# The second layer's modulation made in the first layer's MLP but for twelve columns, on one Trainium2 core

## The chip, the cores and the metric

One Trainium2 chip, one of its cores. The metric is the time of one execution of the kernel on the device, in microseconds (us), lower is better. Shown are the median of three runs and one further execution taken by the hardware profiler.

## The reference, cut to what matters

Two layers over a sequence of 512 frames of 1024 channels, all in float32. Each layer first makes six vectors of 1024 values from a conditioning vector c, the same for all frames; this is the modulation:

```python
c_act = silu(c)
for l in range(2):
    mod = c_act @ ada_w[l] + ada_b[l]                 # 1024 -> 6 * 1024
    sh1, sc1, gt1, sh2, sc2, gt2 = split(mod, 6)
    h = rms_norm(x, norm1_g[l]) * (1 + sc1) + sh1
    ...                                                # projections of h, RWKV-7 scan, pooling, gates
    x = x + gt1 * (mixed @ w_out[l])
    h2 = rms_norm(x, norm2_g[l]) * (1 + sc2) + sh2
    gate, up = split(h2 @ w_gu[l], 2)
    x = x + gt2 * ((silu(gate) * up) @ w_down[l])
return rms_norm(x, final_g)
```

Of these vectors sh1 and sc1 are needed when a layer begins, gt1 at the end of its mixer (everything up to w_out), sh2 and sc2 at the start of its MLP, gt2 at the MLP's end.

## The kernel before, in words

Channels lie on the 128 partitions, frames along the free dimension: eight tiles of 128 x 512 hold x. Every float32 product runs as three TensorE passes with operands split into a high part rounded to fp32r and a low remainder (`block`, L217): weights come as 128 x 1024 tiles of 512 KB (`weights`, L174), loaded by SyncE's queue into `raw` (three buffers), cast on ScalarE to `whi` (L185), and the remainder `wlo` is made either on VectorE (L191) or, with `by_dma`, by ScalarE writing minus raw (L188) and an accumulating transfer from GpSimd's queue (L189).

**The modulation** of one layer is 48 columns of 128 outputs, numbered 0 to 47 (sh1 0 to 7, sc1 8 to 15, gt1 16 to 23, sh2 24 to 31, sc2 32 to 39, gt2 40 to 47). One column is one row load of 512 KB by SyncE's queue (`rows`, L239) and one VectorE multiply-and-sum over 1024 elements with `cact` (`modulation`, L248, L254), which leaves the sum in `mods`. The profile names such an instruction by where its row landed: `row`, `hf`, `ar` or `raw`.

Columns still to be made stand in the list `self.todo`. `some(n)` (L259) is called at chosen places of the program; each call makes the column that has been on its way longest, if as many rows are on their way as there are landing places (`self.land`), and sends for new rows until all places are filled. `flush` makes what is left on the way. The landing places are borrowed from tiles that stand empty at the time: two `ar` tiles in the mixer until head pair 3 begins to fill them, after that `raw` buffers of the weights themselves, two halves of `hf0` in w_out, two tiles `row0` and `row1` in the MLP and the down products.

**Layer 0** begins with its 16 columns of sh1 and sc1. Its mixer makes the next 24, its w_out 6, and its last two are made in its MLP. The MLP (`mlp`, L1234) has two parts. First 19 steps of about 10 us (`seven`, L1178), in which gate and up projections are made as seven half-size products; `some(1)` stands in every third step (L1346). Then the down products, eight products m of 22 blocks (`product`, L1380), whose results go to x at once (`residual`, L367). For m = 1 to 6 `some(1)` stands after every second group of three blocks, three in a product (L1399 to L1406), behind the residual of product m - 1: `tc.issue_after` puts the block's instructions on that instruction's engine, VectorE, behind it in the engine's order. These places take 25 columns, 2 of layer 0 and 23 of layer 1. The constant LATE = 26 allows 26 to be left, and 25 are. The seventh of the eight products is followed by `onward` (L458): the last product in two halves, and between its blocks the norm of the next stage and that stage's first projections, in a TensorE order that is fixed by the program (`pinned`).

**Layer 1's mixer** (`mixer`, L925) puts the left columns back into `todo` (L932). It projects the pool inputs and, for each head pair j = 0 to 3, k, r and v, then the 16 gates. While head pair j is prepared on VectorE, ScalarE and GpSimd (`front`, L621: decay, normalised keys; `back`, L677: value residual, chunk matrices `ar`), TensorE is given the blocks of the projections in between; the table SLOT (L79) says how many blocks follow which part, and its third number where `some(1)` stands: four times in each of the rounds j = 1 to 4. So 17 columns are made here, the last four of them through `raw` buffers. Then `solve` (L737) inverts 64 x 64 triangles on VectorE under 51 blocks of gates, `chain` (L812) runs the scan. Before w_out what exceeds eight columns is made (L1024), and `gains` (L1026) makes 1 + sc2 times the norm's weight. w_out takes 6 columns, the MLP the last 2.

Engines work off their instructions in the order in which the scheduler put them; a DMA queue does the same, so a load that waits for its buffer holds up the loads behind it.

Of the kernel before, what the change touches and what calls it, by code (L numbers as in the profile page):

```python
# [19 lines left out]
P = 128  # L20
# [46 lines left out]


SOME = 1
LATE = 26  # L70

NORM = ((12, 4), (14, 10))

# [44 lines left out]
class Trunk:  # L118
    def __init__(self, ctx, tc, a, out):
        self.ctx, self.tc, self.nc, self.a, self.out = ctx, tc, tc.nc, a, out  # L120
        self.pinned, self.last, self.by_dma = False, None, False
        self.third, self.turn, self.ahead, self.on_way, self.land = None, 0, 1, [], []
        self.count, self.fetched = 0, []
        self.hf, self.exact, self.later = None, False, []
        nc = self.nc
        pool = lambda **k: ctx.enter_context(self.pool(**k))
        self.const = pool(name="const", bufs=1)
        self.wraw = pool(name="wraw", bufs=3)
        self.whl = pool(name="whl", bufs=2)
        self.hp = pool(name="hp", bufs=1)  # L130
        self.psum = pool(name="psum", bufs=4, space=PSUM)
        self.dram = pool(name="dram", bufs=1, space=DRAM)
        self.cst = self.const.tile([P, N_CST], F32, name="cst")
        self.cols = self.const.tile([P, N_COLS], F32, name="cols")
        self.ones = self.const.tile([P, P], F32, name="ones")
        self.mean = self.const.tile([P, 1], F32, name="mean")
        self.eps = self.const.tile([P, 2], F32, name="eps")
        self.mods = [self.const.tile([P, 48], F32, name=f"mods{l}") for l in range(L)]
        self.gsc = [self.const.tile([P, 16], F32, name=f"gsc{l}") for l in range(L)]
        self.omm = [self.const.tile([P, 15], F32, name=f"omm{l}") for l in range(L)]  # L140
        self.omka = [self.const.tile([P, 4], F32, name=f"omka{l}") for l in range(L)]
        self.xs = [self.dram.tile([P, S], F32, name=f"xs{k}") for k in range(KC)]
        self.yb = {
            (n, g): self.dram.tile([P, S], F32, name=f"{n}{g}") for n in ("yh", "yl") for g in range(4)
        }
        self.vf = [self.dram.tile([P, S], F32, name=f"vf{j}") for j in range(NJ)]
        self.hd = {k: self.dram.tile([P, S], F32, name=f"hd{k}") for k in AWAY}
# [26 lines left out]
    def weights(self, src, engine=None, pool=None, pair=None):  # L174

        nc = self.nc
        raw = self.fetched.pop(0) if self.fetched else self.fetch(src)
        if pool is None:
            pool = self.whl
            if self.third is not None:  # L180
                self.turn = (self.turn + 1) % 3
                pool = self.whl if self.turn else self.third
        new = lambda n: pool.tile([P, 1024], F32R, tag=n, name=n)
        hi, lo = pair() if pair else (new("whi"), new("wlo"))
        self.on(nc.scalar, "copy")(hi, raw)  # L185
        self.count += 1
        if self.by_dma and (self.by_dma is True or self.count % self.by_dma):
            nc.scalar.activation(lo, raw, AF.Copy, scale=-1.0)  # L188
            nc.gpsimd.dma_start(lo, src, accum_op=ALU.add)  # L189
        else:  # L190
            self.on(nc.vector, "tensor_tensor")(lo, raw, hi.bitcast(F32), ALU.subtract)  # L191
        return hi, lo
# [66 lines left out]
    def some(self, n):  # L259

        for _ in range(n):
            ahead = max(1, len(self.land))
            self.flush(ahead - 1)
            while self.todo and len(self.on_way) < ahead:
                l, i = self.todo.pop(0)
                self.on_way.append((l, i, self.rows(l, i)))

# [190 lines left out]
    def onward(self, l, which, xs, soon, late, last, head=NORM[0]):  # L458

        self.new_h()
        a, b = HALVES
        self.go(last(a))
        ws, banks = soon(), None
        self.pinned = True
        under = last(b)
        for hs, n in zip(HALVES, (head, NORM[1])):
            self.go(under, n[0])
            rb = self.rstd(hs, lambda: self.go(under, n[1]))  # L470
            self.go(under)
            for k in range(KC):
                self.modulated(l, which, xs[k], rb, k, hs)
                if banks is None:
                    ws += late()
                    banks = self.banked(ws)
            under = self.outer(banks, ws, hs)
        self.soon(AF.Silu if which else AF.Sigmoid)
        self.go(under)
        self.pinned = False  # L480
        return banks


# [85 lines left out]
    def pooled(self, l, zs, st, fill):  # L569

        nc, tc = self.nc, self.tc
        with self.pool(name="pl", bufs=1, side="right") as pl:
            pw = pl.tile([P, 512], F32, name="pw")
            nc.sync.dma_start(pw, self.a["pool_w"][l])
            for g in range(4):
                ps = zs[g]
                if l == 0:
                    self.some(SOME)
                z = pl.tile([P, PAD + S], F32, tag="z", name="z", bufs=2)
                nc.gpsimd.memset(z[:, 0:PAD], 0.0)  # L580
                nc.scalar.copy(z[:, PAD:], ps)
# [343 lines left out]
    def mixer(self, l):  # L925
# [3 lines left out]
        deep = ExitStack()  # L929
        self.third = deep.enter_context(self.pool(name="third", bufs=1, side="right"))  # L930
        self.turn = 2 * l
        self.todo, self.later = self.todo + self.later, []  # L932
        self.pre = right.enter_context(self.pool(name="pre", bufs=13, side="right"))
        sl = right.enter_context(self.pool(name="sl", bufs=1, side="right"))
        sm = low.enter_context(self.pool(name="sm", bufs=1, side="right"))
# [1 line left out]
        rest = range(POOL0 + len(zs), KRV0)  # L937
        st = self.stream([((self.a["w_in"][l, g],), zs.append) for g in rest], [self.m] * 4)
        self.go(st, KC)
        self.g = self.dram.tile([P, NJ, S], F32, tag="g", name="gd")  # L940
        self.krv = {}

# [18 lines left out]
        with ExitStack() as ctx:  # L961
# [26 lines left out]
            for j in range(NJ + 1):  # L988
                self.by_dma = 2 if j in (2, 3) else True
                if l and j == 2:  # L990
                    self.turn, self.count = self.turn + 1, 1
                if j == NJ:
                    self.flush()
                    self.land = []
                steps = [(self.front(l, j) if j < NJ else iter(()), True), (self.back(l, j - 1) if j else iter(()), False)]
                steps = {ahead: g for g, ahead in steps}
                fill = st if j < NJ - 1 else gates
                for n, ahead, some in SLOT[min(j, 1)]:
                    next(steps[ahead], None)
                    self.go(fill, n)  # L1000
                    if some and (l == 0 or j):
                        self.some(1)
            right.close()
            gp = ctx.enter_context(self.pool(name="gp", bufs=1))
# [18 lines left out]
        self.tmp = self.left.enter_context(self.pool(name="t2", bufs=1))  # L1023
        self.some(len(self.todo) - 8)  # L1024
        self.flush()
        self.gains(l, 1)  # L1026
        with ExitStack() as ctx:
            mx = ctx.enter_context(self.pool(name="mx", bufs=1))
            mixed, outs = [], []
# [24 lines left out]
            self.by_dma, self.ahead = False, 1  # L1054
            self.wide = ExitStack()
            hb = self.wide.enter_context(self.pool(name="hb", bufs=1, side="right"))
            self.hb = self.wide.enter_context(self.pool(name="hc", bufs=1, side="right"))
            self.hf = [p.tile([P, KC // 2, S], F32, name=n) for p, n in ((self.hb, "hf0"), (hb, "hf1"))]
            wo = ctx.enter_context(self.pool(name="wo", bufs=3))
            wk = ctx.enter_context(self.pool(name="wk", bufs=4))  # L1060

# [9 lines left out]
            for m in range(KC):  # L1071
                x = self.xp.tile([P, S], F32, tag=f"x{m}", name="x")
                nc.sync.dma_start(x, self.a["x"][m] if l == 0 else self.xs[m])
                self.x.append(x)
            self.land = [self.hf[0][:, 2 * i : 2 * i + 2, :].rearrange("p k n -> p (k n)") for i in range(2)]
            for m in range(5):
                if m == len(outs):
# [1 line left out]
                self.some(1)  # L1079
                self.go(product(m, outs[m], ALL))  # L1080
            self.flush()
            self.land = []
            w = [wout(m, wo) for m in range(5, KC)]

# [149 lines left out]
    def mlp(self, l):  # L1234
# [7 lines left out]
        fp = right.enter_context(self.pool(name="fp", bufs=2, side="right"))  # L1242
        rows = [fp.tile([P, D], F32, name=f"row{i}", bufs=1) for i in range(2)]
        pairs, ws = [], {}
        x = lambda tag: fp.tile(
            [P, S if tag == "x22" else D], F32, tag=tag, name=tag, bufs=1 if tag == "x13" else 2
        )
# [36 lines left out]
        with ExitStack() as ctx:  # L1284
# [40 lines left out]
            for i, m in [*enumerate(HIDDEN)][PLAIN:]:  # L1325
                s, out = begin(m)

                def at(place):
# [14 lines left out]
                        if made:  # L1343
                            nc.gpsimd.dma_start(*made)
                    elif place == 2:
                        if i % 3 == 0 and i < FC - 3:  # L1346
                            self.some(1)
                        step(i + 1)
                    elif place == 3:
# [24 lines left out]
        for k in AWAY:  # L1374
            nc.sync.dma_start(kept[k], self.hd[k])
        t3 = right.enter_context(self.pool(name="t3", bufs=1, side="right"))
        if self.todo:
            self.land = rows

        def product(m, hs):  # L1380
            ps = self.acc() if hs.start == 0 else self.m()
# [15 lines left out]
                yield  # L1397

        for m in range(KC - 1):  # L1399
            stream = product(m, ALL)  # L1400
            for n in range(6):
                self.go(stream, 3)
                if m and n % 2:
                    with tc.issue_after(self.behind.ins):
                        self.some(1)
            self.go(stream)  # L1406
# [1 line left out]
        if l < L - 1:  # L1408
            self.some(len(self.todo) - LATE)
        self.flush()  # L1410
        self.land = []
        self.later, self.todo = self.todo, []
        if l < L - 1:
            self.gains(l + 1, 0)

            pair = self.hb.tile([P, 2, D], F32R, tag="hf0", name="wn", bufs=1)
            both = mr.tile([P, few * S], F32R, tag="hd", name="wn", bufs=1)
            ahead = [
                self.weights_in(l + 1, 2, both=both[:, 0:D]),
# [9 lines left out]
            self.early = dict(enumerate(banks))  # L1429
            right.close()  # L1430
            left.close()
        else:
            self.go(product(KC - 1, HALVES[0]))
            under = product(KC - 1, HALVES[1])
# [141 lines left out]
```

## Time and profile before

| what | before |
|---|---|
| median of 3 runs | 1508.88 us (1507.56 to 1510.38) |
| the profiled execution | 1512.63 us |
| its span, first to last instruction | 1510.8 us |
| around the span | 1.83 us |
| TensorE matmul busy | 1437.5 us, 95% |
| VectorE busy | 1097.3 us, 73% |
| ScalarE busy | 742.9 us, 49% |
| GpSimd busy | 254.5 us, 17% |
| mean granted TensorE clock | 0.988 |
| moved by DMA | 299.28 MB, mean 198 GB/s |

Layer 0's MLP steps lie at about 450 to 640 us of the span, its down products at 640 to 760, layer 1's mixer at 785 to 1100, its w_out to 1125 and its MLP behind that. PE is TensorE, PEld its weight loads, DVE VectorE, ACT ScalarE, POOL GpSimd, SPq SyncE's queue. A row of a timeline gives the start, the duration, and in brackets how long the engine had been idle just before and what ended that. A matmul of 128 x 512 is listed with some 0.39 us but the next starts 0.23 us later: they overlap.

### The profile page before, as it was taken

What the parts mean: (1) busy time and instruction counts of PE and PEld (TensorE: products, weight loads), DVE (VectorE), ACT (ScalarE), POOL (GpSimd) and SP (SyncE); (2) the same over time, 40 slices, a digit from 0 to 9 for tenths busy, and PEclk for the clock granted to TensorE, in tenths of its full rate; (3) what the DMA queues carried; (4) which work ended last, traced back from release to release, by engine and by line L of the source; (5) the groups of instructions that cost most, each with busy time, mean ns of one, the idle gap of its engine ahead of it and who ended that gap; (6) DMA issues with size and microseconds to landing.
All of it is one profiled execution on the core that took longest, in us unless ns stands there. A gap on an engine that the chain in (4) does not pass through costs nothing. (4 is left out here: it accounts for less than half of the span.)

```text
span 1510.8 us, 25366 instructions
## 1 busy us (share of the span) xinstructions
PE 1437.5 (95%) x9986; PEld 1226.7 (81%) x9986; DVE 1097.3 (73%) x1857; ACT 742.9 (49%) x1014; POOL 254.5 (17%) x296
## 2 busy tenths in 40 slices
PE   4999899999999999999999989899999999999997
PEld 2776677777899999988897757677779999998886
DVE  7789869676788888865675796677577888787333
ACT  4376554343446656632346656353434666656221
POOL 1124321110022211100022333111102122110000
PEclk9999999999999999999999999999999999999998
DMA  9478689698739988766726966876975699885332
GB/s 360 152 243 244 194 216 275 156 267 245 227 103 240 233 204 194 190 210 200 241 67 204 237 180 164 242 188 175 298 244 156 179 218 206 182 168 165 92 97 70
DMA packets 112487, 299.28 MB, mean 198 GB/s; under 512 B 12080, under 2 KB 22704, under 8 KB 112368
## 3 DMA queue, kind: packets, MB, share of 16 engines
q1 hardware_dynamic: 89440, 227.93, 46.1%
q0 software_dynamic: 21776, 68.69, 25.2%
q8 instruction: 78, 1.28, 0.3%
q10 hardware_dynamic: 1152, 1.05, 0.2%
q14 instruction: 41, 0.34, 0.1%
HBM read 269.84 MB, written 27.79 MB: 197 GB/s over the span
## 5 line engine op out<-in xcount | busy, mean ns | idle before, releaser
L211 PE MATMUL acc<-hh,whi 128*128 128x512 f32 (+1 forms) x1128 | 398.4, 359 | 5.3 <-ACT hh L364 4.9
L211 PE MATMUL acc<-hh,wlo 128*128 128x512 f32 (+1 forms) x1120 | 385.4, 349 | 13.0 <-DMA wlo<-in_w_in 10.8
L211 PE MATMUL acc<-hl,whi 128*128 128x512 f32 (+2 forms) x1128 | 375.9, 350 | 2.1 <-POOL hl L365 1.4
L185 ACT CAST whi<-raw 128x1024 fp32r<-128x1024 f32 x151 | 157.8, 1048 | 286.2 <-PE acc L211 186.9
L211 PEld LDWEIGHTS acc<-hh,wlo 128*128 128x128 f32 x1120 | 213.8, 191 | 42.7 <-DMA wlo<-in_w_in 12.9
L211 PEld LDWEIGHTS acc<-hh,whi 128*128 128x128 f32 x1128 | 214.9, 191 | 40.8 <-ACT hh L364 7.8
L211 PEld LDWEIGHTS acc<-hl,whi 128*128 128x128 f32 (+1 forms) x1128 | 207.1, 191 | 30.3 <-POOL hl L365 2.5
L191 DVE TENSOR_TENSOR wlo<-raw,whi 128x1024 fp32r<-128x1024 f32 x86 | 104.9, 1227 | 94.1 <-ACT whi L185 93.7
L211 PE MATMUL acc<-f,whi 128*128 128x512 f32 (+1 forms) x304 | 92.2, 386 | 0.0
L211 PE MATMUL m<-tl,f13h 128*128 128x256 f32 x304 | 86.0, 283 | 0.0
L211 PE MATMUL m<-th,f13l 128*128 128x256 f32 x304 | 86.0, 283 | 0.0
L211 PE MATMUL m<-th,f13h 128*128 128x256 f32 x304 | 85.9, 283 | 0.0
L231 ACT CAST f24h<-x 128x1024 fp32r<-128x1024 f32 x38 | 39.9, 1051 | 61.8 <-DVE x L231 61.8
L188 ACT ACTIVATE wlo<-raw 128x1024 fp32r<-128x1024 f32 x65 | 68.4, 1053 | 0.1
L211 PEld LDWEIGHTS acc<-f,whi 128*128 128x128 f32 x304 | 56.2, 188 | 12.3
L254 DVE CUSTOM_DVE_ANT_0 raw<-raw,cact,cols 128x1024 f32<-128x1024 f32 x29 | 39.8, 1384 | 32.4 <-DMA raw<-in_ada 32.3
L1175 POOL DMA_DIRECT2D f22l<-in_w_gu x38 | 32.7, 861 | 168.4 <-ACT f22l L231 160.0
L189 POOL DMA_DIRECT2D wlo<-in_w_in x41 | 35.8, 873 | 149.9 <-ACT wlo L188 149.9
L231 DVE TENSOR_TENSOR f24l<-x,f24h 128x1024 fp32r<-128x1024 f32 x38 | 46.5, 1224 | 18.9 <-ACT f24h L231 18.9
L211 PE MATMUL acc<-f,wlo 128*128 128x512 f32 (+1 forms) x152 | 58.7, 386 | 0.0
L211 PEld LDWEIGHTS m<-th,f13h 128*128 128x128 f32 x304 | 58.4, 192 | 0.0
L211 PEld LDWEIGHTS m<-th,f13l 128*128 128x128 f32 x304 | 58.4, 192 | 0.0
(319 smaller groups left out, 3437.9 us busy)
## 6 DMA issues: line engine op xcount, KB each, us to landing
raw<-in_w_in SPq DMA_DIRECT2D x70, 512.0 KB, 5.3
raw<-in_w_gu SPq DMA_DIRECT2D x50, 512.0 KB, 4.4
raw<-in_w_down SPq DMA_DIRECT2D x44, 512.0 KB, 3.6
wlo<-in_w_in POOLq DMA_DIRECT2D x41, 512.0 KB, 7.7
wlo<-in_w_gu POOLq DMA_DIRECT2D x40, 512.0 KB, 6.4
x<-in_w_gu SPq DMA_DIRECT2D x76, 256.0 KB, 4.2
raw<-in_ada SPq DMA_DIRECT2D x29, 512.0 KB, 5.4
ar<-in_ada SPq DMA_DIRECT2D x28, 512.0 KB, 5.2
```

The costliest lines, as they stand in the source:

```text
L185: self.on(nc.scalar, "copy")(hi, raw)
L188: nc.scalar.activation(lo, raw, AF.Copy, scale=-1.0)
L189: nc.gpsimd.dma_start(lo, src, accum_op=ALU.add)
L191: self.on(nc.vector, "tensor_tensor")(lo, raw, hi.bitcast(F32), ALU.subtract)
L211: i = (tensor.transpose if transpose else tensor.matmul)(*args, **k).ins
L231: return (lambda *a, **k: self.tc.keep_in_program_order(op(*a, **k))) if self.exact else op
L254: self.on(nc.vector, "tensor_tensor_reduce")(out=raw, in0=raw, in1=self.cact, scale=1.0, scalar=self.cols[:, b + i : b + i + 1], op0=ALU.m ...
L1175: nc.gpsimd.dma_start(lo, two[:, b], accum_op=ALU.add)
```

## The change

- LATE becomes 12, and the list of columns is held at 12 throughout layer 0's MLP by a new number `keep`: `some` sends for no row while 12 or fewer are left.
- In the MLP's steps of layer 0 `some(1)` stands in every second step instead of every third (in layer 1 still every third, from step 5 on).
- In the down products it stands after every group of three blocks but the first, five in a product, for m = 1 to 6, and once in m = 0. From m = 1 there are four landing places: the tile `hf1`, whose contents are used up by then, gives two more. So four rows are on their way.
- In `some` the test is rewritten: a call makes one column if all landing places are filled or nothing more may be sent for, then fills the places.
- The twelve left columns go back into `todo` only at w_out of layer 1 (before: at the start of its mixer). The mixer's `some(1)` of layer 1 thus find nothing. `gains(l, 1)` moves behind the columns of w_out.
- Two weight tiles that layer 1's mixer begins with (`rest`) get their `wlo` behind a marked VectorE instruction of `onward`: the modulation of tile 4 of the norm's second half. Their ScalarE cast is free as before, since the order is set on the marked instruction's engine alone.

```diff
-LATE = 26
+LATE = 12
...
         hi, lo = pair() if pair else (new("whi"), new("wlo"))
+        if self.after:
+            with self.tc.issue_after(self.after.ins):
+                nc.scalar.copy(hi, raw)
+                nc.vector.tensor_tensor(lo, raw, hi.bitcast(F32), ALU.subtract)
+            return hi, lo
...
             ahead = max(1, len(self.land))
-            self.flush(ahead - 1)
-            while self.todo and len(self.on_way) < ahead:
+            if len(self.on_way) >= ahead or len(self.todo) <= self.keep:
+                self.flush(max(0, len(self.on_way) - 1))
+            while len(self.todo) > self.keep and len(self.on_way) < ahead:
...
                 self.modulated(l, which, xs[k], rb, k, hs)
+                if k == 4:
+                    middle = self.behind
...
-        self.todo, self.later = self.todo + self.later, []
...
         self.go(st, KC)
+        self.after = None
...
-                    if some and (l == 0 or j):
+                    if some:
                         self.some(1)
...
         self.some(len(self.todo) - 8)
         self.flush()
-        self.gains(l, 1)
...
+            self.todo += self.later
             self.land = [self.hf[0][:, 2 * i : 2 * i + 2, :].rearrange("p k n -> p (k n)") for i in range(2)]
...
             self.flush()
+            self.gains(l, 1)
...
+        self.keep = LATE if l < L - 1 else 0
...
-                        if i % 3 == 0 and i < FC - 3:
+                        if (i + l) % (2 + l) == 0 and i < FC - 3:
                             self.some(1)
...
         for m in range(KC - 1):
+            if m == 1:
+                more = self.hb[1].tile([P, 2, D], F32, tag="hf1", name="rows", bufs=1)
+                self.land = [more[:, 0, :], more[:, 1, :], *self.land]
             stream = product(m, ALL)
             for n in range(6):
                 self.go(stream, 3)
-                if m and n % 2:
+                if n and (m or n > 4):
                     with tc.issue_after(self.behind.ins):
                         self.some(1)
...
+            self.after = self.middle
```

## Rows read from the trace of the kernel before

**Rows 1.** The profile's page, part 1: busy us, share, instructions, of each engine
```profile
PE 1437.5 (95%) x9986; PEld 1226.7 (81%) x9986; DVE 1097.3 (73%) x1857; ACT 742.9 (49%) x1014; POOL 254.5 (17%) x296
```

**Rows 2.** Busy time by stretch, layer 1's mixer: PE, PEld, DVE, ACT, POOL, clock, DMA
```profile
860.00:880.00 20.00, 14.63 (x92) 10.22 (x92) 19.94 (x25) 7.58 (x11) 9.57 (x9) 0.92 0.83 228
...
960.00:980.00 20.00, 13.93 (x54) 10.97 (x53) 18.84 (x36) 7.78 (x9) 3.70 (x5) 0.83 0.95 250
```

**Rows 3.** Timeline of PE, 850 to 975 us: the rows behind its idle times
```profile
861.40 1.16 PE L211 MATMUL m<-kr,bk 64*128 64x128 f32 x16 [3.06 <-DVE sig L691]
...
877.08 2.05 PE L211 MATMUL m<-sig,cst 128*128 128x512 f32 x2 [3.97 <-DVE sig L666]
...
904.55 1.10 PE L211 MATMUL m<-sig,cst 128*128 128x512 f32 x2 [1.26 <-DVE sig L666]
...
942.24 1.16 PE L211 MATMUL m<-kr,bk 64*128 64x128 f32 x14 [1.13 <-DVE ar L707]
...
955.05 0.50 PE L211 MATMUL acc<-hh,wlo 128*128 128x512 f32 x1 [0.50 <-DMA wlo<-in_w_in]
972.32 0.80 PE L211 MATMUL acc<-hh,wlo 128*128 128x512 f32 x1 [6.07 <-DMA wlo<-in_w_in]
```

**Rows 4.** Instructions of L254, 830 to 965 us: duration ns min/median/max, first and last start
```profile
L254 DVE CUSTOM_DVE_ANT_0 ar<-ar,cact,cols x13: 1268/1280/2284, 839.2 to 907.5; 128x1024 f32<-128x1024 f32 x13
...
L254 DVE CUSTOM_DVE_ANT_0 raw<-raw,cact,cols x4: 1283/1284/1286, 931.9 to 959.7; 128x1024 f32<-128x1024 f32 x4
```

**Rows 5.** Timeline of DVE, 851 to 877 us
```profile
851.42 0.69 DVE L688 TENSOR_TENSOR d<-d,sv 128x512 f32<-128x512 f32 x1 [0.52 <-POOL d L687]
857.64 1.29 DVE L254 CUSTOM_DVE_ANT_0 ar<-ar,cact,cols 128x1024 f32<-128x1024 f32 x1 [5.52 <-DMA ar<-in_ada]
...
876.20 0.73 DVE L666 SCALAR_TENSOR_TENSOR sig<-r,cols,k 128x512 f32<-128x512 f32 x1
```

**Rows 6.** Timelines of SyncE's queue, DVE and ACT, 940 to 964 us
```profile
950.40 10.90 SPq L171 DMA_DIRECT2D raw<-in_w_in  x2
...
959.65 1.28 DVE L254 CUSTOM_DVE_ANT_0 raw<-raw,cact,cols 128x1024 f32<-128x1024 f32 x1 [10.53 <-DMA raw<-in_ada]
...
960.72 1.05 ACT L185 CAST whi<-raw 128x1024 fp32r<-128x1024 f32 x1 [5.98 <-DMA raw<-in_w_in]
```

**Rows 7.** Busy time by stretches of 2 us: the seventh number is the granted clock
```profile
878.00:880.00 2.00, 2.00 (x6) 0.77 (x4) 1.97 (x3) 0.00 (x0) 1.17 (x1) 0.50 1.03 200
...
974.00:976.00 2.00, 2.00 (x6) 1.52 (x6) 1.84 (x5) 0.00 (x0) 0.00 (x0) 0.51 1.09 269
```

**Rows 8.** Layer 0's down products: busy time by stretch; L254 there; loads of weights
```profile
655.00:745.00 90.00, 90.00 (x392) 73.09 (x391) 53.01 (x70) 23.00 (x25) 0.00 (x0) 1.00 0.68 226
...
L254 DVE CUSTOM_DVE_ANT_0 row<-row,cact,cols x20: 1275/1280/1287, 655.5 to 744.7; 128x1024 f32<-128x1024 f32 x20
...
raw<-in_w_down SPq DMA_DIRECT2D x18, 512.0 KB, 4.2
```

**Rows 9.** The closest call of those products: timelines of DVE and ACT, 700 to 707 us
```profile
701.23 1.28 DVE L254 CUSTOM_DVE_ANT_0 row<-row,cact,cols 128x1024 f32<-128x1024 f32 x1
...
703.04 1.22 DVE L191 TENSOR_TENSOR wlo<-raw,whi 128x1024 fp32r<-128x1024 f32 x1
...
700.33 1.05 ACT L185 CAST whi<-raw 128x1024 fp32r<-128x1024 f32 x1 [4.37 <-PE acc L211]
...
705.97 1.05 ACT L185 CAST whi<-raw 128x1024 fp32r<-128x1024 f32 x1 [3.98 <-PE acc L211]
```

**Rows 10.** Busy time by stretch: sixteen steps of the MLP in layer 0 (PE, PEld, DVE, ACT, POOL)
```profile
460.00:620.00 160.00, 160.00 (x1342) 160.00 (x1341) 132.72 (x202) 97.56 (x128) 32.10 (x40) 1.00 0.91 212
```

**Rows 11.** Timelines of DVE and ACT around the norm of layer 1's first stage
```profile
761.12 1.23 DVE L191 TENSOR_TENSOR wlo<-raw,whi 128x1024 fp32r<-128x1024 f32 x1
...
784.50 2.00 ACT L185 CAST whi<-raw 128x1024 fp32r<-128x1024 f32 x2 [4.58 <-PE acc L211]
```

More of the change, by code (lines that the diff above doesn't have):

```diff
@@ L123, in __init__ @@
         self.count, self.fetched = 0, []
-        self.hf, self.exact, self.later = None, False, []
+        self.hf, self.exact, self.later, self.keep = None, False, [], 0
+        self.after = None
         nc = self.nc
@@ L480, in onward @@
         self.pinned = False
+        self.middle = middle
         return banks
@@ L576, in pooled @@
                 ps = zs[g]
-                if l == 0:
-                    self.some(SOME)
+                self.some(SOME)
                 z = pl.tile([P, PAD + S], F32, tag="z", name="z", bufs=2)
@@ L939, in mixer @@
         self.go(st, KC)
+        self.after = None
         self.g = self.dram.tile([P, NJ, S], F32, tag="g", name="gd")
@@ L1056, in mixer @@
             hb = self.wide.enter_context(self.pool(name="hb", bufs=1, side="right"))
-            self.hb = self.wide.enter_context(self.pool(name="hc", bufs=1, side="right"))
-            self.hf = [p.tile([P, KC // 2, S], F32, name=n) for p, n in ((self.hb, "hf0"), (hb, "hf1"))]
+            hc = self.wide.enter_context(self.pool(name="hc", bufs=1, side="right"))
+            self.hb = hc, hb
+            self.hf = [p.tile([P, KC // 2, S], F32, name=f"hf{i}") for i, p in enumerate(self.hb)]
             wo = ctx.enter_context(self.pool(name="wo", bufs=3))
@@ L1376, in mlp @@
         t3 = right.enter_context(self.pool(name="t3", bufs=1, side="right"))
-        if self.todo:
-            self.land = rows
+        self.land = rows
         def product(m, hs):
@@ L1410, in mlp @@
         self.flush()
-        self.land = []
+        self.land, self.keep = [], 0
         self.later, self.todo = self.todo, []
@@ L1414, in mlp @@
             self.gains(l + 1, 0)
-            pair = self.hb.tile([P, 2, D], F32R, tag="hf0", name="wn", bufs=1)
+            pair = self.hb[0].tile([P, 2, D], F32R, tag="hf0", name="wn", bufs=1)
             both = mr.tile([P, few * S], F32R, tag="hd", name="wn", bufs=1)
```

## The prediction

> **What bounds the kernel now.** I began with the page's busy times. TensorE's matmuls are busy 95% of the span, VectorE 73% [rows 1]: seen over the whole span TensorE is the limit, and there are only 1510.8 - 1437.5 = 73 us in which it stands still. So the next view was the busy time by 20 us, to see where those lie. Apart from both ends of the span the MLPs and the down products have none, and layer 1's mixer has the largest: 5.4 us of 860 to 880, where VectorE works 19.94 of 20, and 6.1 us of 960 to 980, where the granted clock is 0.83 as well [rows 2]. In these stretches it isn't TensorE that limits.
>
> The timeline of TensorE names each wait [rows 3]. Four end with a VectorE result: 3.06, 3.97, 1.26 and 1.13, together 9.42 us. Two end when an accumulating weight transfer lands: 0.50 and 6.07. All six have the modulation behind them, in two ways. In the first, VectorE itself: 17 columns are made between 839 and 961 us, 13 through `ar` and 4 through `raw` [rows 4], at 1.28 us each when undisturbed, so 17 x 1.28 = 21.8 us of an engine that works in order; besides, it stood 5.52 us before one of them waiting for its row, with the value residual's L688, begun at 851.42, already behind it [rows 5]. The second is SyncE's queue and the weights' buffers: the last four rows occupy `raw`, of which there are three. A weight load spent until 961.3 in the queue (950.40 + 10.90), the column at 959.65 had kept VectorE idle for 10.53, and the cast at 960.72 waited 5.98 for its load [rows 6]. Cast, remainder and accumulation of that weight are what TensorE then waited for until 972.32.
>
> Idle time has a second price here. Behind the 3.97 us gap the granted clock is 0.50, and behind the 6.07 us one 0.51 [rows 7], the lower of two levels, 1.2 GHz of 2.4; behind the 3.06 us gap I saw no fall. At 0.5 from 877.1 to about 880.3 and from 972.3 to 976.0 TensorE does half the work, so it loses about 1.6 and 1.85 us.
>
> **The change, part by part.**
>
> *Out of the mixer.* All 17 columns leave it: VectorE loses 21.8 us, SyncE's queue 17 issues, the DMA engines 17 x 0.524 = 8.9 MB, and the `raw` ring four tenants. Counting calls: before, MLP and down products of layer 0 made 25 columns and left 25; after, eight calls in the steps take 9, one in m = 0 takes 1, the first of m = 1 takes 2, and 26 more reach 38, with 12 left and three calls over. W_out still takes 6, and layer 1's MLP sends for 6 instead of 2. So of the 17, 13 move to layer 0's MLP and 4 to layer 1's.
>
> The first four waits: at 877.08 the producer is L666 at 876.20, and VectorE's run up to it began 5.52 us late at 857.64 [rows 5], with columns ahead of it and inside it. That wait and any two columns gone make 5.52 + 2.56 = 8.1 us, and TensorE asks for 3.06 + 3.97 = 7.0 up to there. Each further wait has more columns removed ahead of it. I count all 9.42 and the 1.6 of clock: 11.0. Next late, should one remain, would be ScalarE's and GpSimd's links of the same head pair.
>
> The last two waits and their clock are 0.50 + 6.07 + 1.85 = 8.4 us. With `raw` for weights alone the load of 950.40 can go when its buffer's weight is done, and the cast would follow TensorE's release of `whi`. But the chain behind the cast stays (ScalarE twice, GpSimd's issue, an accumulation), and the DMA share is 0.95 [rows 2] and 1.03 to 1.09 in parts [rows 7]. Bounds: 0 to 8.4; I take 5.0, nearer the top since the row load is what came last. Solve's VectorE part starts behind the last column and should gain as much as TensorE.
>
> *Into layer 0's down products.* Eleven more columns: 14.1 us of VectorE in 90, where it is busy 53 [rows 8], so some 67; 5.8 MB on top of 226 GB/s, or 64 GB/s, which at the present ratio of share to rate makes 0.68 x 290 / 226 = 0.87. TensorE there is busy all 90 of 90 [rows 8], and GpSimd's queue is empty. What could suffer is a weight's remainder, which VectorE must finish before the next change of weights. In the closest case the casts start at 700.33 and 705.97, the remainder ended at 704.26, 1.7 us ahead, with one column in front of it [rows 9]. A column more in front costs 1.28, still hidden; two more would show 0.9 us. SyncE's queue carries eleven more loads, each possibly waiting for a column, with weight loads behind it; but a weight lands in 4.2 us [rows 8] and has three buffers of 5.6 us each. Bounds 0 to 20 us (all four landed rows in front of one remainder in each of six products, below); I take 0.5, since the columns stand three blocks apart in the program and a remainder comes every eight.
>
> *Into the MLP steps.* Layer 0 makes two more, layer 1 four more, at 1.28. A step has 84 matmuls, so 1342 of them in 160 us make a step of 10.0 us [rows 10]; VectorE's 132.72 less five columns over 16 steps is 7.9 us. With a column it is 9.2, as in every third step already, with TensorE at 160 of 160. Two fall into layer 1's down products, where nothing else was made. Cost 0; the cover is 0.8 us a step, and past it each costs its overhang.
>
> *The two remainders behind the marked instruction.* One, at 761.12, stood among the norm's steps [rows 11] and goes behind the marked one, some 15 us later by the norm's length. TensorE didn't wait there, so nothing is gained; at most its 1.2 us. Behind it only its `raw` buffer's next load is held up, by some 15 us; that weight is cast at 784.50 when TensorE releases a buffer [rows 11], by when it should have landed. I take 0, at worst 2. `gains` of layer 1 moves behind w_out's columns, which ran there before as well: 0.
>
> Sum: 11.0 + 5.0 - 0.5 = 15.5 us. The profiled execution took 1512.6, 3.7 above the median, and would become 1497.1; from the median 1508.9 it is **1493.4 us**.
>
> **The rivals.**
>
> *The weights' chain stays.* TensorE reaches the gates earlier and waits there for the accumulations, since the transfers can't go faster at such shares [rows 2, 7]. Then only the first four waits come back, and some of that is lost again: 6 to 11 us, near 1500. For it: the share. Against: without the four `raw` rows 2.1 MB less go through just before.
>
> *Nothing moves.* A column costs VectorE the same wherever it stands, and with TensorE at 95% the whole-span view leaves no room: within 3 us of 1508.9. The Trainium skill, "Perfetto Trace Analysis", Identifying Performance Opportunities, says that improvement generally comes from the most-contended engine, which by whole-span occupancy is TensorE. Its own advice to look at regimes, and at Tensor by other measures, weakens that. What speaks against this rival: in the mixer TensorE stands and VectorE ends the waits [rows 2, 3]. For it: the 95% [rows 1].
>
> *Slower: the landed rows get in front of the remainders.* All four landed rows are free when the residual of product m - 1 is done. If VectorE's order puts four ahead of the remainder where one stood [rows 9], it is 3 x 1.28 - 1.7 = 2.1 us late; with the fifth as well 3.4. Over six products that is 13 to 20 us, and each such wait may drop the clock. From 3.1 us per product on it decides: 15.5 + 3 is used up. With 3.4 the time would be 1493.4 + 20.4 = 1513.8. Against it: a change of weights comes every 5.6 us, a column every three blocks, and in 90 us not one wait of TensorE.
>
> *The change doesn't do what it says*: by the count above the calls suffice for 38 columns with three to spare, so I give this nothing.
>
> **How the numbers follow.** Forecast 0.62 (11.5 to 20 us less, 1489 to 1497.4); weights' chain 0.22; nothing 0.06; slower 0.06; more than 20 less 0.04, if small waits outside the sum go too. The range reaches from 1488, all of 9.42 + 1.6 + 8.4 = 19.4 and a little more, to 1504, a part of the second case's lower tail (5 us). Left out are nothing, slower and the extremes, some 0.17. One can tell 0.2%, 3 us, from no change: faster 0.90, same 0.04, slower 0.06.
>
> **What would show it.** Right: no L254 between 785 us and w_out; the waits on L691, L666 and L707 gone in layer 1's mixer; the clock whole where it was 0.92; in the down products 31 columns and TensorE without a gap. The second term is right if the wait for `wlo` before solve is under 3 us and its clock dip is gone. Wrong: gaps ended by `wlo` L191 or L185 in the down products, or new waits of similar sum in the mixer ended by ScalarE, GpSimd or accumulating transfers.

## The result, and the profile after

The changed kernel took 1492.22 us in the median (1488.42 to 1493.07, 4 runs) where the kernel before took 1509.63 on the same chip (1507.56 to 1515.65): ratio 0.9873, 95% interval 0.984 to 0.9906. The forecast was 1493.4 us, in the range 1488 to 1504. The profiled execution took 1491.96 us, its span 1490.2.

The page's first part answers to [rows 1]; busy times hardly differ, so the 20.6 us by which the span is shorter are idle time and clock.

```profile
PE 1432.4 (96%) x9986; PEld 1222.4 (82%) x9986; DVE 1096.1 (74%) x1857; ACT 742.7 (50%) x1014; POOL 254.0 (17%) x296
```

Where they came from is read by cutting both executions at the same instructions: ScalarE's activation `soon`, issued once in each norm and before w_out, and the first matmul `m<-tn,ar` of the triangular solve.

| stretch | before, us | after, us |
|---|---|---|
| start to layer 0's MLP | 432.60 | 432.46 |
| layer 0's MLP steps | 211.98 | 212.04 |
| its down products, with the next norm | 135.13 | 135.09 |
| layer 1's mixer up to the solve | 218.2 | 198.7 |
| solve, scan, gates | 108.8 | 108.8 |
| w_out, with the norm behind it | 62.56 | 61.55 |
| the rest | 341.5 | 341.5 |

All but one us lies in layer 1's mixer ahead of the solve; below, "the stage" is this one. The timeline of PE, 785 to 1000 us, has every wait of that stretch in these rows, against those of [rows 3]:

```profile
802.32 0.50 PE L217 MATMUL m<-hh,whi 128*128 128x512 f32 x1 [1.72 <-ACT whi L191]
...
912.98 0.51 PE L217 MATMUL acc<-hh,wlo 128*128 128x512 f32 x1 [1.61 <-DMA wlo<-in_w_in]
...
970.91 0.50 PE L217 MATMUL acc<-hh,wlo 128*128 128x512 f32 x1 [0.18 <-DMA wlo<-in_w_in]
987.38 0.95 PE L217 MATMUL m<-tt,A 32*32 32x32 f32 x49 [0.51 <-issue]
```

None ends with VectorE any more, and the wait for a weight ahead of the solve is 0.18 where it was 6.07. One is new, the 1.61 us for a remainder at 912.98. By stretch, as in [rows 2], the clock is whole, and in the second the DMA share is higher than before (1.03 for 0.95) with hardly a gap:

```profile
860.00:880.00 20.00, 20.00 (x119) 14.64 (x118) 15.42 (x20) 14.62 (x20) 9.59 (x9) 1.00 0.61 128
...
960.00:980.00 20.00, 19.82 (x145) 15.86 (x144) 18.81 (x35) 9.68 (x13) 3.43 (x4) 1.00 1.03 271
```

Where the columns went, layer 0's down products, TensorE still has no gap in 90 us; VectorE went from 53.01 to 63.91, the DMA share from 0.68 to 0.80 [rows 8]. The second and third rows are the columns there, by landing place, in the instructions of L260:

```profile
655.00:745.00 90.00, 90.00 (x391) 73.12 (x390) 63.91 (x90) 22.33 (x25) 0.00 (x0) 1.00 0.80 275
...
L260 DVE CUSTOM_DVE_ANT_0 row<-row,cact,cols x16: 1273/1276/1281, 655.4 to 741.6; 128x1024 f32<-128x1024 f32 x16
L260 DVE CUSTOM_DVE_ANT_0 rows<-rows,cact,cols x14: 1274/1276/1282, 658.9 to 737.0; 128x1024 f32<-128x1024 f32 x14
```

### The profile page after: what moved, and what is told of

Same layout as the page of the kernel before. It is cut to its first block, busy times and chain, and to the rows that moved or that the text cites. A ratio compares the mean times of both kernels' runs of the same rounds, so it can differ in the third digit from the quotient of the medians.

```text
span 1490.2 us, 25379 instructions
## 1 busy us (share of the span) xinstructions
PE 1432.4 (96%) x9986; PEld 1222.4 (82%) x9986; DVE 1096.1 (74%) x1857; ACT 742.7 (50%) x1014; POOL 254.0 (17%) x296
## 5 line engine op out<-in xcount | busy, mean ns | idle before, releaser
L217 PEld LDWEIGHTS m<-tl,f13h 128*128 128x128 f32 x304 | 58.2, 192 | 0.0
```

The costliest lines, as they stand in the source:

```text
L217: i = (tensor.transpose if transpose else tensor.matmul)(*args, **k).ins
```

## The experiments

Twelve kernels, each the changed one with an edit. The kernel before was timed with each group; its medians there lay between 1506.2 and 1507.9 us. The stage is that of each run's profiled execution, the difference of two starts read to 0.1 us. It varied little between executions in which nothing in it was touched: 198.0 to 199.8 us (the changed kernel, e8, e10, e11 and e12).

| run | edit | median, us | ratio, 95% interval | stage, us |
|---|---|---|---|---|
| e1 | 13 columns back (4 fell into the pooled part) | 1498.80 | 0.9939 (0.9917 to 0.9961) | 206.6 |
| e2 | 4 back (all in the pooled part) | 1487.71 | 0.9862 (0.9831 to 0.9894) | 199.6 |
| e3 | 13 multiplications, no loads | 1494.35 | 0.9916 (0.988 to 0.9952) | 205.5 |
| e4 | 13 loads, no multiplications | 1499.55 | 0.995 (0.993 to 0.9969) | 206.7 |
| e5 | 17 back, as before | 1507.17 | 0.999 (0.997 to 1.0011) | 215.3 |
| e6 | 13 back in rounds 1 to 3 | 1498.86 | 0.995 (0.9933 to 0.9967) | 205.8 |
| e7 | 4 back in round 4 | 1491.50 | 0.99 (0.9873 to 0.9927) | 199.9 |
| e8 | down products: five columns at one place | 1491.32 | 0.9896 (0.9873 to 0.9918) | 198.2 |
| e9 | 17 back, 4 of them not in `raw` | 1496.87 | 0.9929 (0.9903 to 0.9955) | 206.8 |
| e10 | layer 0: round 4's columns in the solve | 1496.26 | 0.9937 (0.9914 to 0.9959) | 199.0 |
| e11 | eight left, none in w_out | 1489.76 | 0.9884 (0.986 to 0.9908) | 199.8 |
| e12 | layer 0: round 4's not in `raw`; eight left | 1485.34 | 0.9856 (0.9829 to 0.9883) | 198.0 |

**e1 and e2: one group of columns back.**

```diff
-LATE = 12
+LATE = 25
...
         self.turn = 2 * l
+        self.todo, self.later = self.todo + self.later[:13], self.later[13:]
...
-                    if some:
+                    if some and (l == 0 or 0 < j < NJ):
```

In e2 the numbers are 16 and 4, and the condition `l == 0 or j == NJ`.

> The changed kernel, but 13 columns are made again in rounds 1 to 3 of layer 1's mixer through the ar places, none through raw. Theory (columns on VectorE and their rows end TensorE's waits there): the four waits on VectorE and the first clock dip come back, 9.4 + 1.6 = 11 us, so 8 to 12 us above the changed kernel, nearly all between the end of layer 0's MLP and the solve's first matmuls. Rival (the four rows in raw did nearly all of the harm): under 3 us above it.

> The changed kernel, but 4 columns are made again in round 4 of layer 1's mixer, through the weights' raw buffers, none through ar. Theory: the weight waits before solve and the second clock dip come back, 0.5 + 6.1 + 1.85 = 8.4 us, of which 1.8 still stands in the changed kernel, so 5 to 8 us above it, with a wait of TensorE on wlo of 4 us or more between 920 and 960 us. Rival (a DMA share near 1 made that wait, not the buffers): under 2 us above it.

Both missed their aim. The change also lets `pooled` call `some` in layer 1, so that four columns ran there, through `raw`, at 794 to 817 us: all four of e2, and four of e1's thirteen. What e2 tells is that four columns in the pooled part cost 0.9 us of stage, which is within the scatter above; e1 with nine in rounds 1 to 3 gave back 7.9.

**e3 and e4: VectorE's share and the queue's, one at a time.** Both add work to the changed kernel, in layer 1's rounds 1 to 3, of which nothing is used. e3 runs thirteen multiply-and-sums of `cact` with itself, each written over a landing place, and loads no row:

```diff
-                    if some:
+                    if some and l and 0 < j < NJ:
+                        for _ in range(2 if not self.made else 1):
+                            self.made += 1
+                            nc.vector.tensor_tensor_reduce(
+                                out=self.land[self.made % 2], in0=self.cact, in1=self.cact, ...
+                            )
+                    elif some:
                         self.some(1)
```

e4 sends for thirteen rows there, which nothing reads: in the loop stands `self.rows(l, self.made)` in place of the reduction.

> The changed kernel plus 13 VectorE multiply-and-sums of the conditioning vector with itself at the calls of rounds 1 to 3 in layer 1's mixer, without any row loads. If VectorE's own time is what counted, most of the 11 us of those rounds comes back: 6 to 11 us. If the waiting for rows was it (5.5 us before one of them), 0 to 3 us.

> The changed kernel plus 13 row loads into the ar places at the same calls, without any VectorE work on them. If transfers and SyncE's queue counted, 5 us or more above the changed kernel; if VectorE's time counted, 0 to 2 us.

Either costs about what the whole columns cost (7.1 in e6, below): 6.8 and 8.0 us of stage. Of e3's 6.8 some 1.7 aren't the multiplications': its granted clock was 0.71, 0.50 and 0.93 in the three stretches of 2 us from 798 to 804, ahead of the first of them at 824, which leaves 5.1 by estimate. In e4 VectorE has not one column, and yet TensorE waits for it. The timelines of PE, GpSimd and VectorE there:

```profile
863.08 2.08 PE L217 MATMUL m<-kr,bk 64*128 64x128 f32 x16 [5.67 <-DVE sig L700]
...
859.53 1.26 POOL L696 TENSOR_TENSOR d<-d,v 128x512 f32<-128x512 f32 x1 [11.20 <-DMA d<-vf]
...
860.82 0.69 DVE L697 TENSOR_TENSOR d<-d,sv 128x512 f32<-128x512 f32 x1 [13.82 <-POOL d L696]
```

The release named first, VectorE, is the last link only. The load of `vf` for the value residual was issued at 851.94 behind eight rows and weights in SyncE's queue (its DMA share 1.04 in 840 to 860), GpSimd waited for it, then VectorE, then TensorE. As nothing reads e4's rows, they went out closer together than rows of real columns; the size is of this run, the path is what it shows.

**e5 to e7: the columns where they stood.** `pooled` asks only in layer 0 again; the rest as in e1, with seventeen (LATE = 29, below), thirteen (25, `0 < j < NJ`) and four (16, `j == NJ`).

```diff
+                if l == 0:
-                self.some(SOME)
+                    self.some(SOME)
...
+        self.todo, self.later = self.todo + self.later[:17], self.later[17:]
...
-                    if some:
+                    if some and (l == 0 or j):
```

> The changed kernel with seventeen columns taken back into layer 1's mixer where they stood before: thirteen through the two landing places in ar in rounds 1 to 3, four through the buffers of raw weights in round 4; none in the pooled part. All else of the change stays (marked remainders, four landing places in the down products, more columns in layer 0's MLP). The measure is the stage from the end of layer 0's down products to the first transpose of the triangular solve: 218.2 us before, 198.7 us after. Theory A, that the seventeen columns alone made the whole gain: the stage is back at 216 to 220 us, the waits on sig (3 to 4 us) and the weights' wait of 5 to 6 us ahead of the solve are back, and the kernel is level with the one before (ratio 0.998 to 1.002). Rival B, that part of the gain is another part of the change's doing, since thirteen columns gave back only about 8 us: the stage is at 205 to 210 us, ratio 0.993 to 0.996.

> Thirteen columns taken back through the landing places in ar in rounds 1 to 3, none in the pooled part and none in round 4 (the earlier try let four of its thirteen slip into the pooled part). Theory A by the prediction's terms: the four waits on sig and ar and the clock come back and the weights' waits do not: stage 198.7 + 11.0 = 209.7 us, ratio 0.994. Rival: the two groups of columns work only together (the column steps of rounds 1 to 3 delay VectorE, and only with round 4's raw buffers does the weights' chain wait): the stage is at 204 to 207 us as in the runs with thirteen multiplications or thirteen loads alone.

> Four columns taken back through the buffers of raw weights in round 4 alone (the earlier try had made all four in the pooled part). Theory A by the prediction's terms: the wait of 6 us for the split weights ahead of the solve comes back in most part and no other does: stage 198.7 + 5.0 = 203.7 us, up to 198.7 + 8.4 = 207.1 us. Rival C, the prediction's own, that the weights' chain is set by something else (SyncE's queue, VectorE's lag from the rounds before): four columns alone cost under 1.5 us here, and the rest only comes with the thirteen.

Theory A holds in e5, but for a stage 0.7 us under its 216: with the seventeen back, nothing of the gain is left (0.999, interval 0.997 to 1.0011), so marked remainders, landing places and the rest of the change are together worth no more than that interval allows, some 4.5 us. But the parts are no sum: thirteen cost 7.1 us over the changed kernel's 198.7, four cost 1.2 (little more than the scatter), and both 16.6. The medians say the same: above e8, which was timed in the same group and has the changed kernel's mixer, e6 lies 7.5 us, e7 0.2 and e5 15.9. The 8.3 us that belong to neither alone are mainly the wait for the weights with its clock. PE's waits of e5, of e6 and of e7, 640 to 1010 us (total, times, longest):

```profile
PE acc L217 <- DMA wlo<-in_w_in: 6.3, 1, 6.3
PE m L217 <- DVE sig L676: 5.1, 2, 4.0
PE m L217 <- ACT whi L191: 1.7, 1, 1.7
PE m L217 <- DVE sig L701: 1.1, 1, 1.1
```

```profile
PE m L217 <- DVE sig L676: 5.8, 3, 4.0
PE m L217 <- ACT whi L191: 1.7, 1, 1.7
PE m L217 <- DVE sig L701: 1.0, 1, 1.0
...
PE acc L217 <- DMA wlo<-in_w_in: 0.3, 1, 0.3
```

```profile
PE acc L217 <- DMA wlo<-in_w_in: 3.2, 3, 1.6
PE m L217 <- ACT whi L191: 1.7, 1, 1.7
```

What the four rows do to a weight can be read in e5's timelines of SyncE's queue, VectorE, ScalarE, GpSimd and TensorE:

```profile
944.99 1.65 SPq L251 DMA_DIRECT2D raw<-in_ada  x1
946.73 11.28 SPq L172 DMA_DIRECT2D raw<-in_w_in  x2
...
956.36 1.28 DVE L260 CUSTOM_DVE_ANT_0 raw<-raw,cact,cols 128x1024 f32<-128x1024 f32 x1 [10.27 <-DMA raw<-in_ada]
...
957.36 1.05 ACT L191 CAST whi<-raw 128x1024 fp32r<-128x1024 f32 x1 [6.19 <-DMA raw<-in_w_in]
...
962.04 1.05 ACT L191 CAST whi<-raw 128x1024 fp32r<-128x1024 f32 x1 [2.67 <-DMA raw<-in_w_in]
...
959.66 0.86 POOL L195 DMA_DIRECT2D wlo<-in_w_in  x1 [13.32 <-ACT wlo L194]
...
968.59 0.80 PE L217 MATMUL acc<-hh,wlo 128*128 128x512 f32 x1 [6.26 <-DMA wlo<-in_w_in]
```

The queue's second line is two weight loads (x2). The first goes out at 946.73, right behind the last row, and lands 10.5 us later. The cast of 957.36 waited for it, GpSimd issued its accumulating transfer at 959.66, and with the landing of that, 8.9 us later, TensorE's 6.26 us end. The second stands in the queue until VectorE has read the row, which took 11.2 us to land (9.5 us is the longest such wait of the queue for `mods`). Its cast is the one of 962.04, and TensorE doesn't wait for its remainder. So the weight that was missing is the first, and in e6, without the four rows, its load went out much earlier:

```profile
927.00 0.33 SPq L172 DMA_DIRECT2D raw<-in_w_in  x1
...
947.79 1.04 ACT L191 CAST whi<-raw 128x1024 fp32r<-128x1024 f32 x1
```

There it landed after 6.2 us, and 14.5 us more passed before its cast. Counted from the start of the stage, e5's load goes out 17.2 us later than e6's and takes 4.3 us longer; less those 14.5 us, its cast comes 7.0 us later. The late issue has the rows in it: the weight load ahead of this one, at 937.71, had stood 5.0 us until VectorE read a row, and the last row went out just before it. What makes the landing slow wasn't tried by itself. In e7 the same load, at 934.12, lands after 9.3 us, and TensorE's wait for its remainder is 0.96.

**e8: the slower rival's burst.**

```diff
-                if n and (m or n > 4):
+                if n == 1 and m or n == 5 and not m:
                     with tc.issue_after(self.behind.ins):
-                        self.some(1)
+                        self.some(5 if m else 1)
```

> The five columns of each of layer 0's down products issued at one place, behind one residual, in place of five places spread over it: the most that landed rows can stand in front of the remainders of the down weights. The prediction's slower rival priced this at 20 us if each burst holds TensorE up: stage of the down products 64 to 84 us long where it is 62. By the theory that VectorE has room there (about 15 of 20 us busy) it costs 0 to 3 us.

The down products with the norm took 135.0 us, as with the changed kernel, and TensorE worked 90.00 of 90 there. VectorE's timeline shows the four landed rows in a run:

```profile
701.34 1.22 DVE L197 TENSOR_TENSOR wlo<-raw,whi 128x1024 fp32r<-128x1024 f32 x1
702.48 1.28 DVE L260 CUSTOM_DVE_ANT_0 rows<-rows,cact,cols 128x1024 f32<-128x1024 f32 x1
703.68 1.28 DVE L260 CUSTOM_DVE_ANT_0 row<-row,cact,cols 128x1024 f32<-128x1024 f32 x1
704.89 1.28 DVE L260 CUSTOM_DVE_ANT_0 row<-row,cact,cols 128x1024 f32<-128x1024 f32 x1
706.10 1.28 DVE L260 CUSTOM_DVE_ANT_0 rows<-rows,cact,cols 128x1024 f32<-128x1024 f32 x1
707.30 1.22 DVE L197 TENSOR_TENSOR wlo<-raw,whi 128x1024 fp32r<-128x1024 f32 x1
```

The order has the remainder of 701.34 ahead of them; the next begins at 707.30 and ends at 708.5, before the cast of 709.85 that follows it. Four columns fit between two remainders.

**e9: the four rows out of the ring.** To e5 it adds

```diff
                 if j == NJ:
                     self.flush()
-                    self.land = []
+                    late = [t[:, NJ - 1] for t in (self.bt, self.vt)]
+                    self.land = [late[0].rearrange("p a c t -> p (a c t)"), late[1].rearrange("p c a t -> p (c a t)")]
+                    calls = 0
...
+                    if some and j == NJ:
+                        calls += 1
+                        self.some(1) if calls < 4 else self.flush()
...
+            self.land = []
```

> The run with seventeen columns taken back, but the four of round 4 land in two places of their own (the last quarters of bt and vt, which are written only at that round's end) and not in the three buffers of raw weights; rows, bytes, multiplications and SyncE's commands are as many as there. With thirteen columns back the stage was 205.8 us, with four 199.9, with all seventeen 215.3, so 8.3 us belong to neither alone. Theory A, that these four rows delay the weights by sitting in the ring of three buffers: the stage falls to 204 to 208 us, the wait of 6.3 us for the split weights ahead of the solve falls under 2 us, ratio 0.993 to 0.996. Rival B, that their bytes on the DMA engines, their places in SyncE's queue or VectorE's passes over them do it: the stage stays at 213 to 217 us and the wait at 5 us or more, ratio 0.998 to 1.001.

The stage is 206.8 us, and the wait is gone; PE's waits, 640 to 1010 us:

```profile
PE m L217 <- DVE sig L676: 5.7, 2, 4.7
PE m L217 <- ACT whi L191: 1.7, 1, 1.7
...
PE acc L217 <- DMA wlo<-in_w_in: 0.2, 1, 0.2
```

It separates less than the expectation says, though. Since the new places are empty from the start, the scheduler moved these rows forward, to be made at 848 to 884 us. So the four passes and their bytes, made earlier, cost little: seventeen columns by round 3 cost about what thirteen do (8.1 us against 7.1). What costs 8.5 us is that the four come in round 4 and through the ring. Whether the ring's buffers alone do it, or also the four transfers at that moment, this run leaves open; e5's trace shows both a late issue and a slow landing.

**e10 to e12: can the same be had in layer 0?** Its mixer ran through the same round 4, with waits for weights of 1.84 us at 233.56 and 2.56 at 253.37 in the changed kernel. e10 makes those four columns in the solve:

```diff
-                    if some:
+                    if some and j < NJ:
...
             for _ in solve:
                 self.go(gates, SOLVE[1])
+                if l == 0:
+                    self.some(1)
```

> The changed kernel, and in layer 0's mixer the four columns of round 4 are made in the triangular solve behind that round, where the DMA engines are busy for 0.6 of the time (1.01 to 1.09 in the 30 us before). There the changed kernel still has three waits for the split weights of 4.6 us in all and two dips of the granted clock to 0.83. Theory A carried over (rows in the raw ring delay the weights ahead of the solve): 2 to 5 us faster than the changed kernel, ratio 0.984 to 0.986. Rival: layer 0's stage is bound by the bytes, or the columns now hold up the solve on VectorE: within 1 us of the changed kernel, or slower.

This gave back half of the change's gain (ratio 0.9937 for 0.9873). VectorE's timeline, and PE's behind it:

```profile
247.63 1.28 DVE L260 CUSTOM_DVE_ANT_0 raw<-raw,cact,cols 128x1024 f32<-128x1024 f32 x1 [6.28 <-DMA raw<-in_ada]
...
262.50 0.31 PE L217 MATMUL m<-tn,ar 32*32 32x32 f32 x2 [6.08 <-DVE tn L783]
```

and PE's clock behind that wait, by stretch:

```profile
260.00:270.00 10.00, 5.85 (x102) 4.62 (x104) 9.91 (x7) 5.03 (x6) 0.86 (x1) 0.50 0.90 224
```

The columns got into the middle of the solve's recurrence on VectorE, which stood 6.28 us for a row, and TensorE waits for that recurrence. e11 leaves eight columns for layer 1 and puts them back into the list only behind w_out's five products; e12 is e11 with e9's landing places, which then serve layer 0 alone.

```diff
-LATE = 12
+LATE = 8
...
-            self.todo += self.later
             self.land = [self.hf[0][:, 2 * i : 2 * i + 2, :].rearrange("p k n -> p (k n)") for i in range(2)]
...
             self.land = []
+            self.todo += self.later
...
-                if n and (m or n > 4):
+                if n and (m or n > 3):
```

> The changed kernel with eight columns left for layer 1 in place of twelve: one more in each of layer 0's down products, none in layer 1's output projection, the eight in its MLP. The output projection took 61.6 us with the twelve, the one before 62.6. Expected if the columns there cost anything: 0 to 2 us faster than the changed kernel; if they are hidden: the same; if a sixth column in each down product is too many: slower, in the stage of the down products.

> The changed kernel with two of the runs before put together: layer 0's four columns of round 4 land in bt's and vt's last quarters and not in the ring of raw weights (in layer 1 no column is made there), and eight columns are left for layer 1, none of them in its output projection. If rows in the ring delay the weights in layer 0's mixer too: the stage there from the pooled products to the triangular solve is 179 to 182 us in place of 184.5 (it varied from 178.6 to 184.9 between executions without this edit), its two waits for the split weights just ahead of the solve (1.84 and 2.56 us) and the dips of the granted clock to 0.83 are gone, and the output projection stays at 59.6 us: 3 to 6 us faster than the changed kernel, ratio 0.982 to 0.985. Rival, the stage is bound by the bytes and the projection's 2 us are given back elsewhere: level with the changed kernel, ratio 0.987 to 0.989.

In e11 w_out and its norm took 59.6 us for 61.6, the stage was 1.1 longer, and the time can't be told from the changed kernel's. In e12 w_out took 59.6 us as well, and layer 0's two waits ahead of the solve are gone with the clock whole; in the changed kernel the second of these rows, 250 to 260 us, had 7.44 of 10.00 at a clock of 0.83:

```profile
240.00:250.00 10.00, 10.00 (x45) 8.17 (x44) 9.14 (x26) 4.07 (x7) 1.73 (x2) 1.00 1.05 294
250.00:260.00 10.00, 10.00 (x103) 8.05 (x102) 9.74 (x10) 5.97 (x8) 1.73 (x2) 1.00 0.94 223
```

From the pooled products to the solve that is 180.5 us for 184.5, but the solve to w_out took 110.8 for 108.3, and that first stretch varied from 178.6 to 184.9 without the edit. e12 has the lowest median of all; its interval (0.9829 to 0.9883) overlaps the changed kernel's (0.984 to 0.9906), so a gain over it isn't shown.

## Why the prediction was right

**The bound.** Right: the waits of layer 1's mixer, with the modulation behind them. e5 shows it from the other side, as all of the gain goes when the columns return.

**The first term, 11.0 us, was sized too large.** e6 has these waits by themselves and costs 7.1 us of stage (7.5 by the medians, above e8); in e5 the four waits are down to three, 6.2 us in all, where [rows 3] had 9.42. The step that failed is counting every wait of one profiled execution in full: that execution was 3.7 us above the median, and its stage (218.2 us) was 2.9 longer than e5's with the same columns. Between the two profiled executions the stage did fall by 19.5, as much as all the bounds, 11.0 + 8.4. Its cause was half of it: the text blamed VectorE's passes and, in 5.52 us, the landing of a row. e3 shows that the passes alone do cost 6.8 (5.1 without the dip of the clock), but e4 shows a second path that can be as long, rows ahead of `d<-vf` in SyncE's queue. Taking out only one of the two would then have gained little; that wasn't tried, and e4's rows went out closer together than real ones.

**The second term, 5.0 us of at most 8.4, was sized too small.** From e6 to e5, four rows in the ring cost 9.5 us; e9 gives 8.5 of it back. So the upper end of the bounds was right, but the working behind it was not: it took the queue's line of 950.40 [rows 6] for one load. That line is two, as in e5. The cast of 960.72 waited for the first, which went out at 950.40 and landed 10.2 us later; only the second stood until the row was read, and TensorE's 6.07 us ended with the first one's remainder. So a slow landing had a part in it, beside the late issue. With the rows gone, the accumulation chain behind the cast and the DMA share, for which 3.4 us were held back, cost next to nothing (the share rose to 1.03 and TensorE waited 0.18). What the text missed is that this term depends on the first: without the thirteen the same four cost 1.2 us (e7), as the weights then arrive just in time. The two errors cancel, and that the sum is so near is luck: 11.0 + 5.0 = 16.0 forecast, 16.6 measured between e5 and the changed kernel.

**The down products, -0.5 us** (bounds 0 to 20): 0.0. They made 30 listed columns, not 31. **The MLP steps, 0**: 211.98 became 212.04, VectorE 132.72 [rows 10] became 135.64, with eight columns where five stood. **The marked remainders and `gains`, 0**: e5 bounds all that is left of the change with them. w_out gave 1.0 us that the sum doesn't have, which is within its scatter: 61 to 63 us in the runs that make six columns there.

**The rivals.** *The weights' chain stays* fell with the wait of 0.18. *Nothing moves* fell too, by the 17.4 us between the medians. The Trainium skill, "Perfetto Trace Analysis", Identifying Performance Opportunities, puts the most-contended engine first. By whole-span occupancy that is TensorE at 95%, whose busy time hardly changed here (1437.5 and 1432.4 us), while its waits in one stage did. The Trainium skill's sentence there on regimes is the one that this trace bears out: VectorE was busy 19.94 of 20 us in the mixer's 860 to 880 and 53.01 of 90 in the down products [rows 2, 8]. *Landed rows in front of the remainders* fell even with the burst: four stand in a run, but behind the nearer remainder.

## What to carry to other kernels

Work that can be done at any time belongs where the engine it uses has room, and not in the stage where three engines hand each other results. Nor should its transfers go through the ring that feeds the busiest engine at a moment when that engine has no weight to spare; here the ring and the moment were not told apart. Before pricing a wait by its named releaser, follow that engine's own wait back a link or two, as a load in a shared queue may stand behind it, and see which instruction of a merged line it was. Price two causes in one stage together: removing one of two that each suffice should gain little, and a stream that is just in time alone is late when another comes with it.

## What was not expected of the hardware

The price of a wait in clock differed more than expected. In e10 the granted clock was 0.50, the lower of the two levels, over all of 260 to 270 us, with the waits of 6.08 and 1.66 us before the matmuls of 262.50 and 264.46; behind the 6.26 us of e5 its mean was 0.83 over 960 to 980; e4's 5.67 us had the same 0.83 over 860 to 880. And in e5 the last 512 KB row took 11.2 us to land and the weight load behind it 10.5, where the weights' loads of that size took 5.4 in the median of 925 to 970 us, with a DMA share of 1.03 to 1.08 from 948 to 954 only.
